# Stick-breaking attention: logits one step earlier, running sums split on VectorE, 13 equal steps

## The chip, the cores and the metric

The kernel runs on one core of one Trainium2 chip. The metric is the device time of one execution in microseconds; the median of several executions counts. Five engines work side by side: TensorE (PE, with its weight loads PEld) for matrix products, VectorE (DVE) and ScalarE (ACT) for elementwise work, GpSimd (POOL) for masks, and SyncE (SP), which issues the transfers from memory.

## What is computed

Two decoder layers over 512 tokens of width 2048, in float32. The first layer is sparse softmax attention, the second is stick-breaking attention; each is followed by an output product, a layer norm and a gated embedding. The change lies in the second layer's attention:

```python
q, gate = jnp.split(x @ w_in, [WIDTH_B], axis=-1)
...
z = jnp.einsum('bqngd,bsnd->bngqs', qg, k).astype(jnp.float32) * (HEAD_DIM ** -0.5)
strict = key_pos[None, :] < t[:, None]
log_om = jnp.where(strict, -jax.nn.softplus(z), 0.0)
suffix = lax.cumsum(log_om, axis=log_om.ndim - 1, reverse=True) - log_om
a = jnp.where(strict, jnp.exp(jax.nn.log_sigmoid(z) + suffix), 0.0)
o = jnp.einsum('bngqs,bsnd->bqngd', a.astype(v.dtype), v)
...
return (o * jax.nn.silu(gate)) @ w_o
```

There are 16 query heads in 4 groups; the four heads of a group share one key and value head.

## The kernel before

Activations are kept transposed, features on partitions and tokens along the free axis. Every float32 operand of a product is split into a high and a low part in a reduced format (`split`, L131: ScalarE rounds the high part, VectorE subtracts for the low part), and a product is three matmuls (`mm3`, L135). Weights arrive by transfers into `raw`, are split into `wh` and `wl` two items ahead, and are used by four gate units each.

The second layer's attention runs group by group (`for g in range(4)`, L1344). In each group two streams of work are woven together on TensorE, whose order is the order of the program:

- the **gate product** of the group (`gemm_w`), 64 units of three matmuls into banks 0 to 3; at every fourth unit the next weight item is split;
- **`sticks(g, Q)`** (L1241), the attention. A unit u = (i, kb) is the 128 queries of block i for all four heads against key block kb; there are ten units, (0,0), (1,1), (1,0), (2,2), (2,1), (2,0), (3,3), (3,2), (3,1), (3,0), from the diagonal (kb = i) back to key block 0.

For a unit, `logits` (L1252) makes z = K Q on TensorE, then softplus: for kb > 0 VectorE copies z to `a`; ScalarE takes Abs, Exp and Ln in `wk`; VectorE adds into `sp`. A diagonal unit is masked on GpSimd (`strict`) and split into `sh` and `sl` at once; any other unit waits for the total of the unit before it. `weights` (L1284) multiplies `sh` and `sl` with a triangle of ones. For kb > 0 the sums go into the bank `later`, VectorE adds them to the copy of z (`a`), and `carry` (L1274) adds the total's row of `later` into `sp` of unit u + 1, which is then split; for kb = 0 the sums are added onto z in its own bank (L1297). ScalarE takes the exponential, a diagonal unit is masked, and the result is split into one of two pairs `A`. `values` (L1305) multiplies with V into the bank `o`, and after kb = 0 ScalarE copies `o` out.

The loop at L1313 makes 12 steps: in step s the logits of unit s, the weights of unit s - 1, the values of unit s - 2, with a `yield` after each. `interleave` (L57) runs a share of gate units after each yield: 52 units over 34 yields in groups 1 to 3, behind a lead of 8; 46 over 28 in group 0, of which 18 units have run already. Four extra yields in step 1 hold back the first weights.

The order on TensorE is written out; on the other engines a scheduler orders instructions by its own estimate of when each is ready. Where `pinned` is set (through `paced`, L325), `keep_in_program_order` ties an instruction to the one traced just before it on the same engine: it is issued after that one, while instructions that are not pinned may still be put between or ahead. Background pieces from the list `bg` are run one after a gate unit and are pinned: in groups 0 to 2 the splits of the next group's queries (`split_scaled`, L1208, `c<-f` in the profile), in group 0 also the pieces of `restore`.

Of the kernel before, what the change touches and what calls it, by code (L numbers as in the profile page):

```python
# [10 lines left out]
F32 = mybir.dt.float32  # L11
F32R = mybir.dt.float32r
I32 = mybir.dt.int32
AF = mybir.ActivationFunctionType
ALU = mybir.AluOpType
# [31 lines left out]
def run(gen):  # L47
    for _ in gen:
        pass


def steps(gen, n):
    for _ in range(n):
        next(gen, None)


def interleave(main, n_main, fill, n_fill, lead=0):  # L57

    steps(fill, lead)
    done = 0  # L60
    for i, _ in enumerate(main, 1):
        steps(fill, n_fill * i // n_main - done)
        done = n_fill * i // n_main
    run(fill)
# [13 lines left out]
def trunk_kernel(  # L78
# [39 lines left out]
    act, dve, pool = (Paced(e) for e in (nc.scalar, nc.vector, nc.gpsimd))  # L118
# [9 lines left out]
    def bank(i, name="ps"):  # L128
        return psum.tile([128, 512], F32, name=name, tag=f"bank{i}")

    def split(hi, lo, src, eng=dve):  # L131
        act.activation(hi, src, AF.Copy)
        eng.tensor_tensor(lo, src, hi.bitcast(F32), ALU.subtract)
# [155 lines left out]
    def gemm_w(items, get, banks, n=512, order=range(NK)):  # L289

        for i, kb in enumerate(order):
            wh, wl = next(items)
            x = get(kb)
            for j, out in enumerate(banks):
                a, b = j * 128, min(n, (j + 1) * 128)
                mm3(out[: b - a], (wh[:, a:b], wl[:, a:b]), x, i == 0, i == len(order) - 1)
                yield
# [27 lines left out]
    def paced(fn, *args):  # L325
        was, pinned[0] = pinned[0], True
        fn(*args)
        pinned[0] = was
# [4 lines left out]
    def pumped_at(gen, when):  # L333
        for i, _ in enumerate(gen):
            if bg and i in when:
                one()
            yield

    def pumped(gen, every=1):

        for i, _ in enumerate(gen):
            if bg and i % every == 0:
                one()
            yield
# [199 lines left out]
    for k in (4, 5, 6, 7, None, 0, None, 1, 2, 3):  # L544
        if k is None:
            first = 4 * (units[-1][1] == 0)
# [113 lines left out]
    def first_pair(banks):  # L660
        for k2 in range(NK // 2):
            for outs, get in zip(banks, (late_plain, plain)):
                for kb in (2 * k2, 2 * k2 + 1):
                    wh, wl = next(items)
                    for j, out in enumerate(outs):
                        s = slice(j * 128, (j + 1) * 128)
                        mm3(out, (wh[:, s], wl[:, s]), get(kb), kb == 0, kb == NK - 1)
                        yield
# [7 lines left out]
    gemm = first_pair((banks, kbanks))  # L676
    steps(gemm, 48)
    gemm = pumped(gemm, 2)
# [26 lines left out]
    gemm = gemm_w(items, late_plain, banks)  # L705
# [41 lines left out]
    def split_queries(g):  # L747
        Q = []
        for h in range(4):
            q = tuple(pkv.tile([128, T], F32R, name=f"q{s}", tag=f"q{s}", bufs=4) for s in "hl")  # L750
            split(*q, F[g][:, h])
            Q.append(q)
        return Q
# [55 lines left out]
    Q = split_queries(0)  # L809
# [59 lines left out]
    for g in range(4):  # L869
        banks = mm_banks("g")  # L870
        interleave(attend(g, Q), 36, gemm_w(items, plain, banks), 50 - 6 * (g == 0), lead=8 + 6 * (g == 0))
        if g < 3:
            Q = split_queries(g + 1)
        for h in range(4):
            sg = pb.tile([128, T], F32, name="sg", tag="sg", bufs=3)
# [286 lines left out]
    Q, A = ([tuple(spots[n : n + 2]) for n in where] for where in ((10, 12, 16, 18), (20, 22)))  # L1162
# [7 lines left out]
    with tc.tile_pool(name="sp", bufs=1) as sp:  # L1170
        Kf, Vf = shared
        banks = [bank(b, "k") for b in range(4)]
        gemm = gemm_w(kitems, plain, banks, order=PAIRS)
# [11 lines left out]
        for n, dst in enumerate((Vf, *F)):  # L1185
            M = product_banks(4 - n)
            gemm = pumped_at(gemm_s(items, C3, M), (13, 20, 27, 34, 41, 53, 65, 77, 89, 101))
# [18 lines left out]
    px = pc_.enter_context(ss(name="px", bufs=1))  # L1206
# [16 lines left out]
    def log_exp():  # L1223
        tc.keep_in_program_order(act.preload_act_table_set("natural_log_exp_and_others"))

    def work():
        return px.tile([128, 512], F32, name="wk", tag="wk", bufs=4)

    def strict(ap, i):
        v = ap.rearrange("p (h q) -> p h q", h=4)  # L1230
# [10 lines left out]
    def sticks(g, Q):  # L1241
        units = [(i, kb) for i in range(4) for kb in range(i, -1, -1)]
        state = {}
        waiting = {}
        out = {}

        def parts_of(sp):
            parts = tuple(px.tile([128, 512], F32R, name=f"s{s}", tag=f"s{s}", bufs=2) for s in "hl")
            split(*parts, sp)
            return parts  # L1250

        def logits(u):  # L1252
            i, kb = units[u]
            z = bank(4 + u % 2, "z")
            ks = slice(kb * 128, (kb + 1) * 128)
            mm3(z, [k[:, ks] for k in K[g]], Q[i], True, True)
            e = work()
            sp = px.tile([128, 512], F32, name="sp", tag="sp", bufs=2)
            if kb:

                copy = px.tile([128, 512], F32, name="a", tag="a", bufs=3)
                dve.tensor_copy(copy, z)
            act.activation(e, z, AF.Abs)
            act.activation(e, e, AF.Exp, scale=-1.0)
            act.activation(e, e, AF.Ln, bias=1.0)
            dve.scalar_tensor_tensor(sp, z, 0.0, e, ALU.max, ALU.add)
            z = copy if kb else z
            if kb == i:
                strict(sp, i)
                state[u] = z, parts_of(sp)  # L1270
            else:
                waiting[u] = z, sp

        def carry(u, total):  # L1274

            z, sp = waiting.pop(u)
            if units[u][1] % 2:
                dve.tensor_tensor(sp[0:1], sp[0:1], total[0:1], ALU.subtract)
            else:
                rows = slice(96, 128)  # L1280
                dve.scalar_tensor_tensor(sp[rows], total[rows], ident[rows, 127:128], sp[rows], ALU.mult, ALU.add)
            state[u] = z, parts_of(sp)

        def weights(u):  # L1284
            i, kb = units[u]
            z, parts = state[u]
            a = z if kb else work()
            if kb:
                later = bank(6, "later")
                for n, p in enumerate(parts):  # L1290
                    pe.matmul(later, down if kb % 2 else tri, p, start=n == 0, stop=n == 1)
                dve.tensor_tensor(a, z, later, ALU.subtract if kb % 2 else ALU.add)
                carry(u + 1, later)
                act.activation(a, a, AF.Exp)
            else:
                for n, p in enumerate(parts):
                    pe.matmul(z, tri, p, start=False, stop=n == 1, skip_group_check=True)  # L1297
                act.activation(a, z, AF.Exp)
            if kb == i:
                strict(a, i)  # L1300
            parts = A[u % 2]
            split(*parts, a)
            state[u] = parts

        def values(u):  # L1305
            i, kb = units[u]
            if kb == i:
                out[i] = bank(7, "o")
            mm3(out[i], [v[:, g * 128 : (g + 1) * 128] for v in V[kb]], state.pop(u), kb == i, kb == 0)
            if kb == 0:  # L1310
                act.activation(F[g][:, :, i * 128 : (i + 1) * 128], out[i].rearrange("p (h q) -> p h q", h=4), AF.Copy)

        for s in range(12):  # L1313

            done = [i for n, (i, kb) in enumerate(units) if kb == 0 and s == max(n + 3, 0 if g else 8)]
            if g < 3:
                bg.extend(lambda i=i: split_scaled(g + 1, i) for i in done)
            for fn, u in ((logits, s), (weights, s - 1), (values, s - 2)):
                if 0 <= u < 10:
                    fn(u)  # L1320
                    yield
                if g and s == 1 and fn == logits:
                    for _ in range(4):
                        yield

    log_exp()

# [7 lines left out]
    gemm = pumped(chunk)  # L1335
    first = sticks(0, Q)
    for n in (9, 1):
        steps(gemm, n)
        steps(first, 1)
    bg.extend(lambda i=i: split_scaled(0, i) for i in (2, 3))  # L1340
    steps(gemm, 8)
    gemm = pumped(chunk, 2)

    for g in range(4):  # L1344
        if g:
            log_exp()
            banks = mm_banks("g")
            gemm = pumped(gemm_w(items, plain, banks))
        if 0 < g < 3:
            bg.append(lambda g=g: split_keys(g + 1))  # L1350
        if g:
            interleave(sticks(g, Q), 30 + 4, gemm, 52, lead=8)
        else:
            interleave(first, 30 - 2, gemm, 64 - 18)
        drain()
        if g < 3:
            split_scaled(g + 1, 3)
        for h in range(4):
            sg = work()
            act.activation(sg, banks[h], AF.Silu)  # L1360
            dve.tensor_tensor(F[g][:, h], F[g][:, h], sg, ALU.mult)
    pk_.close()
# [55 lines left out]
```

## Time and profile before

| | |
|---|---|
| median of three runs | 1887.99 us (1886.46 to 1888.04) |
| profiled execution | 1886.27 us, span 1884.1 us |
| granted TensorE clock | 1.000 |
| TensorE busy | 1860.9 us, 99% |
| VectorE busy | 1222.8 us, 65% |
| ScalarE busy | 944.0 us, 50% |
| stick-breaking stage | about 1234 to 1510 us of the span |

In the rows shown below, a line names the engine, the source line, the operation, and output and inputs by the program's tile names; [..] behind a row is the idle time of that engine before it and what ended it. Most VectorE and ScalarE instructions bear the line of a helper (L111), so they are told apart by their tiles: `sp<-z,wk` is the softplus sum, `sp<-later,ident,sp` and `sp<-sp,later` are the carry, `a<-a,later` the add of the sums, `c<-a` the split of the weights into `A` (and `c<-wk` for kb = 0). Matmuls overlap, so their pace is read from start to start. In the rows by stretch the columns are the stretch, its length, and busy time (with instruction counts) of PE, PEld, DVE, ACT, POOL, then the granted clock, the share of the transfer engines and GB/s.

### The profile page before, as it was taken

The page shows a single profiled execution, that of the slowest core. Times are in us where ns is not written, and L with a number is a line of the kernel's source. Part 1 is how long each engine was busy: PE and PEld are TensorE (multiplying, and loading weights), DVE is VectorE, ACT ScalarE, POOL GpSimd, SP SyncE. Part 2 cuts the span into 40 slices and gives each one's busy share as a digit, 9 for nine tenths or more (in the row PEclk, how much of TensorE's full clock was granted, in tenths as well). Part 3 has the DMA queues.
Part 4 walks back from the last instruction along what each step waited for, and adds up shares of the span by engine and source line. Part 5 has one row for each costly group of instructions (what it writes and reads, how often), then busy time and mean ns, then how long its engine had stood idle before and what let it go on. Part 6 is the DMA issues. An engine that isn't in the chain of part 4 may idle for free.

```text
span 1884.1 us, 24811 instructions
## 1 busy us (share of the span) xinstructions
PE 1860.9 (99%) x9181; PEld 1575.1 (84%) x9181; DVE 1222.8 (65%) x2363; ACT 944.0 (50%) x1712; POOL 27.4 (1%) x48
## 2 busy tenths in 40 slices
PE   9999999999999999999999999999999999999998
PEld 8898888888888888888888999977777788888887
DVE  5768678567565455675377888877766645567534
ACT  3546423455554432474245444477877743246422
POOL 0000000000000000000000000000000000000000
PEclk9999999999999999999999999999999999999999
DMA  6442333312222532333343333322122152242333
GB/s 196 126 123 62 96 101 90 101 56 68 73 66 63 182 98 78 123 101 115 103 145 112 105 99 107 107 85 78 56 68 60 53 190 94 79 129 90 123 101 112
DMA packets 111178, 189.21 MB, mean 100 GB/s; under 512 B 8528, under 2 KB 29008, under 8 KB 111056
## 3 DMA queue, kind: packets, MB, share of 16 engines
q1 hardware_dynamic: 111056, 187.62, 32.3%
q8 instruction: 72, 1.18, 0.3%
q14 instruction: 50, 0.41, 0.1%
HBM read 179.21 MB, written 8.39 MB: 100 GB/s over the span
## 4 chain that ended last, share of the span: by engine, by line
PE 95%; DVE 3%; ACT 2%; issue 0%; DMA 0%; SPq 0%; POOL 0%; DVEq 0%
PE g L136 12%; PE g L137 12%; PE g L138 12%; PE o L138 7%; PE o L136 7%; PE o L137 7%; PE m L136 4%; PE m L137 4%; PE m L138 4%; PE q L136 3%; PE q L137 3%; PE q L138 3%; PE k L138 2%; PE k L137 2%; PE k L136 2%; PE iq L138 1%
## 5 line engine op out<-in xcount | busy, mean ns | idle before, releaser
L111 ACT ACTIVATE wh<-raw 128x512 fp32r<-128x512 f32 (+3 forms) x685 | 397.8, 581 | 703.6 <-PE g L137 235.5
L111 DVE TENSOR_TENSOR wl<-raw,wh 128x512 fp32r<-128x512 f32 (+3 forms) x685 | 432.0, 631 | 472.8 <-ACT wh L111 457.6
L136 PE MATMUL g<-xh,wh 128*128 128x512 f32 x1024 | 404.1, 395 | 0.1
L138 PE MATMUL g<-xh,wl 128*128 128x512 f32 x1024 | 399.9, 391 | 0.0
L137 PE MATMUL g<-xl,wh 128*128 128x512 f32 x1024 | 399.6, 390 | 0.0
L138 PEld LDWEIGHTS g<-xh,wl 128*128 128x128 f32 x1024 | 192.3, 188 | 41.0
L136 PEld LDWEIGHTS g<-xh,wh 128*128 128x128 f32 x1024 | 192.5, 188 | 37.4 <-ACT wk L111 0.7
L137 PEld LDWEIGHTS g<-xl,wh 128*128 128x128 f32 x1024 | 192.6, 188 | 37.1
L138 PE MATMUL o<-xh,wl 128*128 128x512 f32 x512 | 199.4, 389 | 0.0
L136 PE MATMUL o<-xh,wh 128*128 128x512 f32 x512 | 199.3, 389 | 0.0
L137 PE MATMUL o<-xl,wh 128*128 128x512 f32 x512 | 199.3, 389 | 0.0
L138 PEld LDWEIGHTS o<-xh,wl 128*128 128x128 f32 x512 | 96.1, 188 | 20.4 <-DVE wl L111 0.5
L136 PEld LDWEIGHTS o<-xh,wh 128*128 128x128 f32 x512 | 96.1, 188 | 19.9
L137 PEld LDWEIGHTS o<-xl,wh 128*128 128x128 f32 x512 | 96.1, 188 | 19.8
L136 PE MATMUL q<-xh,wh 128*128 128x512 f32 x256 | 99.7, 389 | 0.0
L138 PE MATMUL q<-xh,wl 128*128 128x512 f32 x256 | 99.6, 389 | 0.0
L137 PE MATMUL q<-xl,wh 128*128 128x512 f32 x256 | 99.6, 389 | 0.0
L111 ACT ACTIVATE sh<-st 128x512 fp32r<-128x512 f32 x80 | 49.7, 624 | 44.3 <-DVE st L111 44.2
L111 DVE TENSOR_TENSOR sl<-st,sh 128x512 fp32r<-128x512 f32 x80 | 55.2, 690 | 13.9 <-ACT sh L111 13.9
L111 DVE TENSOR_TENSOR xl<-f,xh 128x512 fp32r<-128x512 f32 x80 | 54.3, 686 | 12.6 <-ACT f L111 12.3
L138 PEld LDWEIGHTS q<-xh,wl 128*128 128x128 f32 x256 | 48.1, 188 | 10.1
L136 PEld LDWEIGHTS q<-xh,wh 128*128 128x128 f32 x256 | 48.1, 188 | 10.0
(294 smaller groups left out, 3342.9 us busy)
## 6 DMA issues: line engine op xcount, KB each, us to landing
raw<-w_in_a SPq DMA_DIRECT2D x95, 512.0 KB, 3.6
raw<-w_in_b SPq DMA_DIRECT2D x64, 512.0 KB, 3.8
raw<-w_ple_gate SPq DMA_DIRECT2D x52, 512.0 KB, 3.6
raw<-w_o_a SPq DMA_DIRECT2D x24, 512.0 KB, 3.8
raw<-w_o_b SPq DMA_DIRECT2D x24, 512.0 KB, 3.7
raw<-w_kv_b SPq DMA_DIRECT2D x16, 512.0 KB, 3.8
raw<-w_ple_gate SPq DMA_DIRECT2D x24, 256.0 KB, 2.9
f<-xT SPq DMA_DIRECT2D x4, 1024.0 KB, 6.6
```

The costliest lines, as they stand in the source:

```text
L111: ins = method(*args, **kw)
L136: pe.matmul(out, a[0], b[0], start=start, stop=False)
L137: pe.matmul(out, a[0], b[1], start=False, stop=False)
L138: pe.matmul(out, a[1], b[0], start=False, stop=stop)
```

## The change

- The loop makes 13 steps: logits of unit s, weights of unit s - 2, values of unit s - 3. Every step has three yields, whether a part runs or not; step 1 has two extra yields in groups 1 to 3 in place of four. The gate units are spread over 39 + 2 yields in groups 1 to 3 and over 39 - 6 in group 0.
- z goes into bank 4 for kb > 0, into bank 5 for kb = 0, and into bank 6 for the first unit; `sp` reads the copy of z where there is one. Buffers: `wk` 3 in place of 4, `sp` 3 in place of 2, `a` 4 in place of 3; the silu of the gate uses the tag `a`.
- In `carry` the high part is a VectorE copy in place of ScalarE's, right behind the sum, and the low part follows. Diagonal units are still split by `split`.
- `carry` comes ahead of the add into `a`, and both are paced.
- With 13 steps the background split of query block 3 is also listed in step 12; the call after the group stays.

```diff
     def work():
-        return px.tile([128, 512], F32, name="wk", tag="wk", bufs=4)
+        return px.tile([128, 512], F32, name="wk", tag="wk", bufs=3)
...
         def logits(u):
             i, kb = units[u]
-            z = bank(4 + u % 2, "z")
+
+            z = bank(4 if kb else 5 if u else 6, "z")
...
-            dve.scalar_tensor_tensor(sp, z, 0.0, e, ALU.max, ALU.add)
+            dve.scalar_tensor_tensor(sp, copy if kb else z, 0.0, e, ALU.max, ALU.add)
             z = copy if kb else z
             if kb == i:
                 strict(sp, i)
-                state[u] = z, parts_of(sp)
+                state[u] = z, new_parts()
+                split(*state[u][1], sp)
...
-            state[u] = z, parts_of(sp)
+            hi, lo = new_parts()
+            dve.tensor_copy(hi, sp)
+            dve.tensor_tensor(lo, sp, hi.bitcast(F32), ALU.subtract)
+            state[u] = z, (hi, lo)
...
-                dve.tensor_tensor(a, z, later, ALU.subtract if kb % 2 else ALU.add)
-                carry(u + 1, later)
+                paced(carry, u + 1, later)
+                paced(dve.tensor_tensor, a, z, later, ALU.subtract if kb % 2 else ALU.add)
                 act.activation(a, a, AF.Exp)
...
-        for s in range(12):
+        for s in range(13):
 
             done = [i for n, (i, kb) in enumerate(units) if kb == 0 and s == max(n + 3, 0 if g else 8)]
...
-            for fn, u in ((logits, s), (weights, s - 1), (values, s - 2)):
+            for fn, u in ((logits, s), (weights, s - 2), (values, s - 3)):
                 if 0 <= u < 10:
                     fn(u)
+                yield
+                if g and s == 1 and fn == logits:
                     yield
-                if g and s == 1 and fn == logits:
-                    for _ in range(4):
-                        yield
+                    yield
...
     for n in (9, 1):
         steps(gemm, n)
-        steps(first, 1)
+        steps(first, 3)
...
-            interleave(sticks(g, Q), 30 + 4, gemm, 52, lead=8)
+            interleave(sticks(g, Q), 39 + 2, gemm, 52, lead=8)
         else:
-            interleave(first, 30 - 2, gemm, 64 - 18)
+            interleave(first, 39 - 6, gemm, 64 - 18)
...
-            sg = work()
+            sg = px.tile([128, 512], F32, name="sg", tag="a", bufs=4)
```

More of the change, by code (lines that the diff above doesn't have):

```diff
@@ L1245, in sticks, with new_parts @@
         out = {}
[L1247 to L1250, printed above, removed]
+        def new_parts():
+            return tuple(px.tile([128, 512], F32R, name=f"s{s}", tag=f"s{s}", bufs=2) for s in "hl")
         def logits(u):
             i, kb = units[u]
-            z = bank(4 + u % 2, "z")
+            z = bank(4 if kb else 5 if u else 6, "z")
             ks = slice(kb * 128, (kb + 1) * 128)
@@ L1257, in logits @@
             e = work()
-            sp = px.tile([128, 512], F32, name="sp", tag="sp", bufs=2)
+            sp = px.tile([128, 512], F32, name="sp", tag="sp", bufs=3)
             if kb:
-                copy = px.tile([128, 512], F32, name="a", tag="a", bufs=3)
+                copy = px.tile([128, 512], F32, name="a", tag="a", bufs=4)
                 dve.tensor_copy(copy, z)
```

## The prediction

> **What bounds the kernel now.** I read the page first, for the engine that fills the span.
>
> ```profile
> span 1884.1 us, 24811 instructions
> PE 1860.9 (99%) x9181; PEld 1575.1 (84%) x9181; DVE 1222.8 (65%) x2363; ACT 944.0 (50%) x1712; POOL 27.4 (1%) x48
> ```
>
> TensorE is 99% busy, so an edit pays or costs only by the TensorE waits it takes away or makes. The second view, who waited for whom on TensorE, puts nearly all waits into the stick-breaking stage (columns: us in total, times, longest):
>
> ```profile
> PE z L1297 <- DVE sl L111: 5.3, 8, 1.1
> PE later L1291 <- ACT sh L111: 5.0, 5, 1.8
> PE later L1291 <- DVE sl L111: 4.2, 9, 1.2
> PE z L1297 <- ACT sh L111: 1.4, 2, 0.7
> ```
>
> All four end at a high or low part of the running sums (`sh`, `sl`): 15.9 us. The third view gives busy times by stretch, here one stretch for each of the four K/V groups:
>
> ```profile
> 1233.70:1307.00 73.30, 67.96 (x288) 53.03 (x287) 57.25 (x94) 58.19 (x106) 5.78 (x10) 1.00 0.26 80
> 1307.00:1374.70 67.70, 63.89 (x271) 49.98 (x271) 47.76 (x74) 52.59 (x92) 6.19 (x8) 1.00 0.20 62
> 1374.70:1442.30 67.60, 63.96 (x273) 50.34 (x272) 47.19 (x73) 52.51 (x91) 6.20 (x8) 1.00 0.20 63
> 1442.30:1510.00 67.70, 63.67 (x272) 50.13 (x271) 45.21 (x70) 50.60 (x89) 5.80 (x8) 1.00 0.20 63
> ```
>
> The fourth, TensorE's timeline, gives the pace:
>
> ```profile
> 1399.66 0.40 PE L136 MATMUL g<-xh,wh 128*128 128x512 f32 x1
> ...
> 1404.44 0.39 PE L1291 MATMUL later<-sh,down 128*128 128x512 f32 x1
> 1404.99 0.50 PE L1291 MATMUL later<-sl,down 128*128 128x512 f32 x1 [0.16 <-DVE sl L111]
> 1405.33 0.40 PE L136 MATMUL g<-xh,wh 128*128 128x512 f32 x1
> ```
>
> Between the first two rows stand 21 starts (gate 3, values 3, gate 6, logits 3, gate 6): 4.78 / 21 = 0.2276 us each. After a wait the next start comes 0.34 later, so a wait costs about 0.11 more. By the code a group has 272 matmuls (64 gate units of 3; 10 units with 3 logits, 2 sums, 3 values): 61.9 us at this pace, against 67.7. The first stretch has 288 records, 65.5 of 73.3. The stage loses 7.8 + 5.8 + 5.7 + 5.8 = 25.1 us. No cure of these waits can bring more.
>
> **The change, part by part.** *Less cover in a step.* Gate units per step fall from 3 x 52/34 = 4.6 to 3 x 52/41 = 3.8. With 8 matmuls of its own, a step on TensorE shrinks from 4.95 to 4.4 us: every chain that runs from one step to the next has half a microsecond less.
>
> *The pins.* `carry` and the add into `a` are now paced: each VectorE instruction of theirs goes behind the VectorE instruction traced just before. The trace of before shows what such a pin does, since the background split of the next group's queries (`c<-f`) carries one:
>
> ```profile
> 1403.04 0.69 DVE L111 TENSOR_TENSOR wl<-raw,wh 128x512 fp32r<-128x512 f32 x1 [0.53 <-ACT wh L111]
> 1403.65 0.68 DVE L111 SCALAR_TENSOR_TENSOR c<-f,c 128x512 fp32r<-128x512 f32 x1
> 1404.25 0.69 DVE L111 TENSOR_TENSOR sl<-sp,sh 128x512 fp32r<-128x512 f32 x1
> ...
> 1406.41 0.69 DVE L111 SCALAR_TENSOR_TENSOR sp<-z,wk 128x512 f32<-128x512 f32 x1 [0.20 <-ACT wk L111]
> 1407.14 0.76 DVE L111 SCALAR_TENSOR_TENSOR sp<-later,ident,sp 32x512 f32<-32x512 f32 x1
> ```
>
> Here a weight split `wl` was traced between the logits and the `c<-f`, so `c<-f` sits behind `wl` and ahead of that step's `sp`. Where no `wl` lies between, `c<-f` sits right behind the logits' last instruction, as the next block shows in its last row. It is a diagonal unit from its third logits matmul on (copy, Abs, `sp`, GpSimd's mask, `sh`, `sl`):
>
> ```profile
> 1392.08 0.39 PE L138 MATMUL z<-c,c 128*128 128x512 f32 x1
> 1392.64 0.69 DVE L111 COPY a<-z 128x512 f32<-128x512 f32 x1
> 1393.49 0.58 ACT L111 ACTIVATE wk<-z 128x512 f32<-128x512 f32 x1
> 1395.77 0.69 DVE L111 SCALAR_TENSOR_TENSOR sp<-z,wk 128x512 f32<-128x512 f32 x1 [1.25 <-ACT wk L111]
> 1396.59 0.96 POOL L1232 TENSOR_SCALAR_AFFINE_SELECT sp<-sp 128x512 f32<-128x512 f32 x1 [5.38 <-DVE sp L111]
> 1397.59 0.63 ACT L111 ACTIVATE sh<-sp 128x512 fp32r<-128x512 f32 x1 [1.33 <-POOL sp L1232]
> 1398.59 0.68 DVE L111 TENSOR_TENSOR sl<-sp,sh 128x512 fp32r<-128x512 f32 x1
> 1399.19 0.68 DVE L111 SCALAR_TENSOR_TENSOR c<-f,c 128x512 fp32r<-128x512 f32 x1
> ```
>
> So `sp` starts 3.7 us and `sl` 6.5 us after that matmul. In the changed step the order of tracing is logits(s), fill, weights(s-2) with its pinned carry. In steps 3 and 6 the logits are of a diagonal unit (i=2, i=3), weights is unit 1 or 4, and both have a carry. No weight split falls between: a split is traced at every fourth gate unit, and counting 52i/41 from a lead of 8 the gate units there are numbers 21, 22 and 33. So the carry, whose total lies ready at 1.1 to 1.6 us, waits until 6.5 + 0.6 = 7.1, the 0.6 being the spacing of independent VectorE operations above. Behind it wait the high part, the low part, the add into `a`, and then TensorE twice: for the next sums and for the values. Before, no carry fell into these steps (they had unit 2 or 5, with kb = 0), and none was pinned.
>
> *The high part on VectorE.* The row of such a cast, and of what leaves ScalarE:
>
> ```profile
> L111 DVE CAST xh<-raw 128x512 fp32r<-128x512 f32 x1 | 0.4, 419 | 0.0
> ...
> L111 ACT ACTIVATE sh<-sp 128x512 fp32r<-128x512 f32 x40 | 24.9, 623 | 9.2 <-POOL sp L1232 6.6 <-DVE sp L111 2.5
> ```
>
> 24 of the 40 move: 24 x 0.42 = 10 us more VectorE work in the whole stage, which has 15 to 20 us a group free; no cost by itself. Chain of a carry: 0.76 + 0.03, cast 0.42 + 0.03, low part 0.69, and 0.05 to TensorE (`sl` ends at 1404.94, its matmul starts at 1404.99): 1.98 us. The dependent step costs 0.73 (1406.41 to 1407.14), the independent one 0.60. The Trainium skill ("VectorE: DVE Perf Modes", The DRAIN you can't avoid) has it that a semaphore between chained VectorE operations costs nothing extra; the rows differ by 0.13, and by the page the three-operation chain would be 0.4 shorter and the time some 3 us less. I take the rows.
>
> *The add into `a` behind carry and parts.* From the add to the values' low part:
>
> ```profile
> 1389.10 0.69 DVE L111 TENSOR_TENSOR a<-a,later 128x512 f32<-128x512 f32 x1 [0.81 <-PE later L1291]
> 1389.82 0.63 ACT L111 ACTIVATE a<-a 128x512 f32<-128x512 f32 x1
> 1390.58 0.63 POOL L1232 TENSOR_SCALAR_AFFINE_SELECT a<-a 128x512 f32<-128x512 f32 x1 [3.68 <-ACT a L111]
> 1391.25 0.63 ACT L111 ACTIVATE c<-a 128x512 fp32r<-128x512 f32 x1 [0.19 <-POOL a L1232]
> 1391.91 0.69 DVE L111 TENSOR_TENSOR c<-a,c 128x512 fp32r<-128x512 f32 x1
> ```
>
> 0.72 + 0.76 + 0.67 + 0.66 + 0.69 + 0.05 = 3.55 with GpSimd's mask, 0.77 less without (`ea` straight to the split).
>
> *Site A, steps 3 and 4.* From the third logits matmul: carry 7.1, low part 8.35, its matmul at 9.1, `a` at 8.95, the second matmul of values(1) at 12.5 (unit 1 is diagonal: masked). On TensorE that is matmul number 33, due at 7.5. Delay 5.0, of it 2.7 at the sums and 2.3 at the values, + 0.1. In groups 1 and 2 a background split stands between (as 1399.19 does): + 0.6.
> *Site C, steps 6 and 7.* Values(4) unmasked: ready at 11.7, matmul 30 due at 6.8: 4.9 + 0.1. Step 5's carry, behind its `sp`, delays values(3) by some 2 us, but after the logits of step 6, so inside this sum.
> *Site D, steps 8 to 10.* In groups 1 to 3 a weight split lies between, the carry starts at about 2.6, and only the late `a` shows: 0.4 to 0.5 three times, 1.5 with restarts.
> Group 0 (1.39 units a yield): 5.1 at A; at C a restore adds 0.4 but three more matmuls cover: 4.7; at D no split lies between: 2.5.
> Sum 12.3 + 12.3 + 12.2 + 11.6 = 48.4 us. Some 2 us of waits at the first logits stay; the old 25.1 go: + 25 us if nothing else queues in these chains. In the rows above `wl` and `c<-f` stood in front of `sl`, so I add one foreign VectorE operation (0.6) and one on ScalarE (0.5) at each of 8 sites: + 9, an estimate. Net + 34 us. Bounds: if `sl` comes 0.6 sooner, with less on ScalarE, and nothing queues, + 20; if one of the two sites in every group hides, with its queueing, about + 10; with twice the queueing, + 43.
>
> *At nothing:* all z in bank 4 (Abs ends at 1394.07, 2.0 us after the matmul; the next z comes 3.4 or more after it; were Abs 1.4 later, TensorE would wait); `wk`, `a`, `sp` buffers (each next use is a step or more behind the release); the second split of query block 3 in step 12 (one ScalarE and one VectorE operation in three groups, under the next group's 8 gate units, 5.5 us; uncovered, 2 us for each group).
>
> The profiled execution took 1886.27 us; the median shown is 1887.99, 1.7 above. 1887.99 + 34 = 1922.
>
> **The rivals.** *Faster: carries go at once.* If the carry comes when its total lands (the diagonal's chain ends early enough, or the pin doesn't hold it), a carry is done by 1.6 + 2.0 = 3.6 us, against matmuls due at 5.5 or later: the old waits vanish, and site D and the first logits stay, 4 x 1.5 + 2 = 8 of 25.1. Time 1888 - 17 = 1871. It decides where `sl` of units 3 and 6 ends before about 4 us. For it: it is just the slack that a second step ahead gives, and ScalarE loses 24 operations. Against: `sp` alone starts at 3.7, and `c<-f` at 1399.19 shows the pin holding.
> *No change:* delays at A and C half as long, 1888.
> *Slower still: a cold TensorE.* Waits of 2.7 to 3.4 us at A and C, where the longest now is 1.8. The start of the trace shows a cold pace:
>
> ```profile
> 4.42 0.52 PE L137 MATMUL iq<-xl,wh 128*128 128x384 f32 x1
> 4.75 0.52 PE L138 MATMUL iq<-xh,wl 128*128 128x384 f32 x1
> ...
> 6.46 0.34 PE L136 MATMUL iq<-xh,wh 128*128 128x384 f32 x1
> 6.64 0.34 PE L137 MATMUL iq<-xl,wh 128*128 128x384 f32 x1
> ```
>
> 0.33 against 0.18, until 5.7 us. A stretch of 4 us at that pace loses 2 us: over four sites + 8, over eight + 16: 1930 to 1938. Against: the granted clock is 1.00 in all four stretches. The Trainium skill ("TensorE: Matmul & The Clock Gate", HAM oscillation) warns of idle gaps over about 3.4 us; these waits reach that edge, and no run here shows one.
>
> **How the numbers follow.** Forecast 0.80, colder 0.05, no change 0.04, faster 0.11. A measurement of this kernel can tell about 0.2% (3.8 us). Slower is 0.85. The range 1898 to 1943 runs from the bound of one hidden site a group (1888 + 10) over twice the queueing (1931) and the cold case (1938) to a little of both; outside lie the faster and the unchanged case and a little of the forecast's own tail.
>
> **What would show it.** Right: in the list of TensorE's waits new rows for `o` (values) waiting on `c`, and for `z` L1297 with waits over 2 us, some 3 to 5 us a group each; on VectorE's timeline the carry right behind the diagonal's `sl`; the group stretches at 72 to 78 us instead of 67.7; DVE CAST at 0.42. Wrong: stretches of 63 to 66 us, or carries that start within 1 us of their total in steps 3 and 6.

## The result and the profile after

The changed kernel takes 1946.13 us (median of 4 runs, 1945.98 to 1947.78) against 1887.74 us: a ratio of 1.0313, 95% interval 1.0295 to 1.0331. It is 58 us slower; + 34 was forecast and 1946 lies just above the range's end of 1943. The page's head, with the row of the granted clock in 40 slices:

```profile
span 1944.4 us, 24849 instructions
PE 1886.6 (97%) x9181; PEld 1585.8 (82%) x9181; DVE 1235.3 (64%) x2390; ACT 932.7 (48%) x1691; POOL 25.6 (1%) x48
...
PEclk9999999999999999999999999999989899999999
```

The span grew by 60.3 us, VectorE's work by 12.5. TensorE has the same instructions and is "busy" longer: the clock row shows why in two slices. TensorE's waits:

```profile
PE o L136 <- ACT c L111: 17.8, 15, 2.2
PE z L1300 <- DVE sh L111: 14.6, 4, 4.0
PE later L1294 <- DVE a L111: 8.6, 5, 3.7
PE o L137 <- DVE c L111: 6.5, 15, 0.7
PE z L1300 <- DVE sl L111: 2.7, 6, 0.6
```

Here are the rows that were forecast as a sign: values waiting on `c` (24.3 us in 30 waits) and the sums at L1300 with waits of 3 to 4 us. These five lines are 50.2 us; the four of before were 15.9. The stretches of the four groups, the first cut at its first gate unit, the others 2 to 3 us ahead of their first logits, as before:

```profile
1233.70:1322.30 88.60, 73.14 (x291) 55.14 (x291) 60.53 (x101) 55.49 (x101) 5.96 (x10) 0.96 0.22 66
1322.30:1406.00 83.70, 71.12 (x273) 53.44 (x272) 51.55 (x82) 50.13 (x87) 5.41 (x8) 0.92 0.17 51
1406.00:1489.00 83.00, 71.01 (x275) 53.62 (x274) 50.75 (x80) 49.94 (x86) 5.41 (x8) 0.92 0.17 51
1489.00:1572.00 83.00, 71.65 (x278) 54.25 (x277) 49.56 (x78) 48.54 (x85) 5.41 (x8) 0.92 0.17 51
```

83 us a group in place of 67.7 (72 to 78 was forecast), and a granted clock of 0.92 to 0.96 in place of 1.00. At half clock for the missing share, that is 88.6 x 0.08 + 249.7 x 0.16 = 47 us of the stage.

Sites A and C are the prediction's two places of a group where a carry falls behind a diagonal's logits. Site A of the last group shows the whole mechanism. VectorE's timeline from the diagonal's low part on:

```profile
1510.10 0.69 DVE L111 TENSOR_TENSOR sl<-sp,sh 128x512 fp32r<-128x512 f32 x1 [1.18 <-ACT sh L111]
1510.80 0.76 DVE L111 SCALAR_TENSOR_TENSOR sp<-later,ident,sp 32x512 f32<-32x512 f32 x1
1511.59 0.69 DVE L111 SCALAR_TENSOR_TENSOR sp<-a,wk 128x512 f32<-128x512 f32 x1
1512.20 0.42 DVE L111 CAST sh<-sp 128x512 fp32r<-128x512 f32 x1
1512.66 0.69 DVE L111 TENSOR_TENSOR sl<-sp,sh 128x512 fp32r<-128x512 f32 x1
1513.38 0.69 DVE L111 TENSOR_TENSOR a<-a,later 128x512 f32<-128x512 f32 x1
```

And TensorE's, from the diagonal unit's last logits matmul on:

```profile
1503.27 0.39 PE L138 MATMUL z<-c 128*128 128x512 f32 x1
...
1505.08 0.39 PE L1294 MATMUL later<-sl,down 128*128 128x512 f32 x1
...
1512.68 0.79 PE L1300 MATMUL z<-sh,tri 128*128 128x512 f32 x1 [3.13 <-DVE sh L111]
1513.40 0.79 PE L1300 MATMUL z<-sl,tri 128*128 128x512 f32 x1
...
1517.85 0.80 PE L137 MATMUL o<-c,c 128*128 128x512 f32 x1
1518.44 0.63 PE L138 MATMUL o<-c,c 128*128 128x512 f32 x1
1518.87 0.63 PE L136 MATMUL g<-xh,wh 128*128 128x512 f32 x1
1519.30 0.63 PE L137 MATMUL g<-xl,wh 128*128 128x512 f32 x1
```

The total was on its way at 1505.08; the carry starts at 1510.80, right behind the diagonal's `sl`, 7.5 us after the logits (forecast 7.1). A foreign `sp` slips in behind it, so the three are not adjacent. At all eight sites A and C of this trace the carry stands behind the diagonal's `sl`, 6.4 to 8.3 us after the logits. The values' second matmul comes at 14.6 where 7.5 was its turn. And the last rows are 0.43 apart in place of 0.23: the gate products, which wait for nothing, run at half pace. The stretch of that place:

```profile
1511.80:1522.00 10.20, 7.74 (x16) 5.05 (x17) 4.10 (x7) 3.00 (x6) 0.63 (x1) 0.50 0.17 54
```

A clock of 0.50 for 10.2 us, from just before the end of a 3.1 us wait. I split every start in the stage, from the first gate unit (1233.7) to just behind the last group's values, by what it lost against 0.2276 us. Starts behind a wait lost 22.1 us before and 65.0 after (+ 42.9), starts at half pace with no wait 0 and 16.8, all others 4.2 and 4.0. That is 59.5 of the 60.3 us. By place, over the four groups:

| place (from, to) | before | after |
|---|---|---|
| site A (logits of unit 3 to values of unit 1) | 4.6 | 29.8 |
| site C (logits of unit 6 to values of unit 4) | 2.6 | 28.5 |
| behind C to the last values | 14.6 | 20.1 |
| between A and C | 2.4 | 6.2 |
| the rest (first logits, group ends) | 2.1 | 1.2 |

### The profile page after: what moved, and what is told of

Read it like the earlier page. It is cut to its first block, busy times and chain, and to the rows that moved or that the text cites. A ratio compares the mean times of both kernels' runs of the same rounds, so it can differ in the third digit from the quotient of the medians.

```text
span 1944.4 us, 24849 instructions
## 1 busy us (share of the span) xinstructions
PE 1886.6 (97%) x9181; PEld 1585.8 (82%) x9181; DVE 1235.3 (64%) x2390; ACT 932.7 (48%) x1691; POOL 25.6 (1%) x48
## 5 line engine op out<-in xcount | busy, mean ns | idle before, releaser
L138 PEld LDWEIGHTS o<-xh,wl 128*128 128x128 f32 x512 | 96.1, 188 | 20.1 <-DVE wl L111 0.2
L111 DVE TENSOR_TENSOR xl<-f,xh 128x512 fp32r<-128x512 f32 x80 | 54.3, 686 | 12.5 <-ACT f L111 12.2
L111 ACT ACTIVATE wk<-z 128x512 f32<-128x512 f32 x56 | 33.1, 591 | 51.6 <-DVE a L111 22.9
L137 PEld LDWEIGHTS q<-xl,wh 128*128 128x128 f32 x256 | 48.0, 188 | 10.1
```

The source lines that it names most:

```text
L111: ins = method(*args, **kw)
L137: pe.matmul(out, a[0], b[1], start=False, stop=False)
L138: pe.matmul(out, a[1], b[0], start=False, stop=stop)
```

## The experiments

Each ratio is against the kernel before, run on the same chip.

**The pins alone.** The changed kernel without them:

```diff
-                paced(carry, u + 1, later)
-                paced(dve.tensor_tensor, a, z, later, ...)
+                carry(u + 1, later)
+                dve.tensor_tensor(a, z, later, ...)
```

> The changed kernel without the two pins: carry and the add into a are no longer tied to the VectorE instruction traced before them; all else stays (13 steps, high part on VectorE, carry ahead of the add). Pins theory: with no pin the carry starts within about 1 us of its total in steps 3 and 6 instead of behind the diagonal's sl, TensorE's waits fall from 50.9 us to under 15, the clock stays at 1.00, and the time is 1868 to 1885. Rival, VectorE overloaded by the 24 casts or too little cover in 13 equal steps: the waits stay, 1935 to 1950. In between (1890 to 1930) both have a part.

Measured: 1894.49 us, 1.0035 (1.0022 to 1.0049). 52 of the 58 us go with the pins, so neither the casts nor the cover make the loss. But the time is above what the theory gave, and still 0.35% slower than before. Most of TensorE's waits are now at L1300:

```profile
PE z L1300 <- DVE sl L111: 11.8, 8, 1.9
PE z L1300 <- DVE sh L111: 5.0, 5, 2.1
PE o L137 <- DVE c L111: 1.9, 3, 1.5
```

VectorE's timeline at site A of the last group says what they wait for:

```profile
1466.87 0.76 DVE L111 SCALAR_TENSOR_TENSOR sp<-later,ident,sp 32x512 f32<-32x512 f32 x1
1467.66 0.69 DVE L111 TENSOR_TENSOR a<-a,later 128x512 f32<-128x512 f32 x1
1468.27 0.69 DVE L111 TENSOR_TENSOR wl<-raw,wh 128x512 fp32r<-128x512 f32 x1
1468.87 0.68 DVE L111 SCALAR_TENSOR_TENSOR sp<-a,wk 128x512 f32<-128x512 f32 x1
1469.55 0.69 DVE L111 COPY a<-z 128x512 f32<-128x512 f32 x1
1470.15 0.44 DVE L111 CAST sh<-sp 128x512 fp32r<-128x512 f32 x1
```

The carry goes at once, but the order that the scheduler then chose puts four other operations between it and its high part. That is a cost of its own, which the forecast's faster rival left out. The clock has a part in it too: the span is 8.6 us longer than before, and by the count above the starts at half pace lost 5.8 us.

**Weights ahead of logits**, the pins kept:

```diff
-            for fn, u in ((logits, s), (weights, s - 2), (values, s - 3)):
+            for fn, u in ((weights, s - 2), (logits, s), (values, s - 3)):
```

> The changed kernel with weights(s-2) traced ahead of logits(s) in each step; the pins stay. Pins theory: the pin now sits behind work of the step before, not behind this step's logits, so the waits at z and o vanish and the time is 1866 to 1885. Rival, the pinned chain of carry, high, low and add is itself too long: the values still wait on c, 1900 to 1930. Rival, too little cover: 1935 or more.

Measured: 1894.82 us, 1.0041 (1.0026 to 1.0056), in none of the three ranges. Pins, casts, depth and cover are those of the changed kernel; only what is traced in front of the carry differs, and 51 us go. So the harm is the tie to the diagonal's logits. What is left is mostly the values:

```profile
PE o L137 <- DVE c L111: 9.0, 12, 1.2
PE o L136 <- ACT c L111: 3.2, 6, 1.1
```

**The pins in the old order** (12 steps, add first, then carry, both paced).

> The kernel before with the two pins alone (add first, then carry, both paced; 12 steps, ScalarE makes the high part). Pins theory in its narrow form, that a pin costs only where it ties a carry to a diagonal unit's logits: in the 12-step order no carry falls into such a step, so within 6 us of before, 1882 to 1894. Rival, pins cost in any order: 1900 or more.

Measured: 1904.59 us, 1.0091 (1.0076 to 1.0106). The narrow theory fell: pins cost 17 us in the 12-step order too. The waits:

```profile
PE later L1291 <- ACT sh L111: 15.4, 12, 2.1
PE later L1291 <- DVE sl L111: 3.9, 13, 0.4
```

There the add into `a` is tied behind `sp` of the same step, and the carry behind the add; so a pin behind `sp`, which waits for a chain of its own, costs too. Some 10 of the 17 us are starts at half pace.

**Zero matmuls in TensorE's waits.** They add a product with zeros:

```diff
+                if u == 2:
+                    warm(z, 16)
                 for n, p in enumerate(parts):
                     pe.matmul(z, tri, ...)
...
+            if u == 4:
+                warm(out[i], 8)
```

> The changed kernel with matmuls of a zero matrix added, 16 ahead of the sums of unit 2 and 8 ahead of the values of unit 4 in each group: they add nothing to the result and stand where TensorE waits now (3.6 us and 1.8 us at 0.23 each). Cold-clock theory, that about 20 us of the loss is TensorE at half clock after these waits: the waits are filled, the clock rows go back towards 1.00 and the time falls to 1922 to 1932. Rival, the slow pace has another cause (weights or operands late): no shorter than 1944, or longer by what of the 22 us of zero matmuls finds no room.

Measured: 1943.41 us, 1.0296 (1.0279 to 1.0313): neither theory's number. 96 zero matmuls are 21.9 us of added work, and only 18 us of waits (65.0 to 47.0) took them in. The clock did go up, over the stage from 0.93 to 0.96:

```profile
1233.70:1572.00 338.30, 302.95 (x1220) 231.93 (x1219) 213.24 (x342) 205.16 (x358) 22.19 (x34) 0.96 0.18 55
```

Starts at half pace lost 9.8 us in place of 16.8. The sum - 18.0 + 21.9 - 7.0 + 0.5 = - 2.6 is the 2.7 measured. So filling waits does keep the clock, but by 7 us, not by the 14 or more that I had expected.

**Add first, logits first.** The changed kernel with its two paced calls turned round:

```diff
-                paced(carry, u + 1, later)
                 paced(dve.tensor_tensor, a, z, later, ...)
+                paced(carry, u + 1, later)
```

> The changed kernel with the order of the two paced calls turned round: add into a first, then carry (logits still first). Theory of the prediction: the add and the carry both wait behind the diagonal's sl; the add first frees the values by 1.3 us but the sums come 0.6 later, so the second wait of each site shrinks and the first stays: 1915 to 1935, waits 40 to 50 us in place of 65. If the order of these two is the main thing: under 1900. If it is nothing: 1940 to 1950.

Measured: 1929.63 us, 1.0224 (1.0210 to 1.0238), as forecast. No wait at the values remains in the list; those at the sums grow:

```profile
PE z L1300 <- DVE sh L111: 27.2, 8, 5.3
PE later L1294 <- DVE sl L111: 6.7, 8, 1.1
```

So the add's place behind the carry is worth 16 us, and the tie to the logits holds without it.

**The high part back on ScalarE**, pins kept (`act.activation(hi, sp, AF.Copy)` in `carry`).

> The changed kernel with the carry's high part back on ScalarE, the pins kept (carry, low part, add). Rival theory, the 24 casts overload VectorE or ScalarE was the better place: well under 1946, 1900 to 1930. Pins theory alone: the carry still waits behind the diagonal's sl, so the waits stay, and a hop to ScalarE and back adds 0.3 us a site: 1940 to 1955.

Measured: 1944.72 us, 1.0303 (1.0289 to 1.0317). The casts are not the cause; the 24 of them cost VectorE 10.0 us in the changed kernel, as forecast:

```profile
L111 DVE CAST sh<-sp 128x512 fp32r<-128x512 f32 x24 | 10.0, 418 | 0.1
```

**The carry free, the rest of its chain tied.** High part, low part and add stay paced, the first instruction isn't.

> The changed kernel with the carry's first instruction free and the high part, low part and the add still pinned one behind the other. Pins theory in its exact form, that the tie of the first instruction to the logits does the harm and the ties within the chain none: as without pins or better, 1880 to 1896. Rival, the ties of the high part, low part and add hold back the values: 1900 to 1930.

Measured: 1930.62 us, 1.0225 (1.0209 to 1.0240), a miss: only 15 us go, about where the rival had it. VectorE's timeline at site A of the last group:

```profile
1495.93 0.76 DVE L111 SCALAR_TENSOR_TENSOR sp<-later,ident,sp 32x512 f32<-32x512 f32 x1
...
1499.21 0.42 DVE L111 CAST sh<-sp 128x512 fp32r<-128x512 f32 x1
1500.47 1.29 DVE L111 TENSOR_TENSOR sl<-sp,sh 128x512 fp32r<-128x512 f32 x2 [0.85 <-ACT sh L111]
1501.68 0.68 DVE L111 TENSOR_TENSOR a<-a,later 128x512 f32<-128x512 f32 x1
```

The carry starts 2.3 us after the logits (1493.64), so the first tie did hold it. But a pin only says "behind", not "next to": the high part was put 3.3 us later, the low part beside the diagonal's, and the add, tied behind the low part, still comes at 8 us. The run without pins has its high and low part at the same places of this site (5.6 and 7.4 us after the logits); only its add goes at 3.1 us. By these rows the tie of the add behind the low part makes most of the 36 us between the two runs. Why the scheduler puts the high part there in both, with nothing in the trace to wait for, stays open.

**Both repairs: weights first and add first, paced.**

> Weights ahead of logits as in the earlier run, and the add into a ahead of carry again; both paced. If what was left there (12 us of values waiting on c) comes from the add standing behind carry, high and low part, those waits go: waits under 16 us, 1872 to 1882, faster than before. Rival, the pinned chain as a whole or VectorE's load holds it: 1890 to 1900, as with weights first alone.

Measured: 1887.58 us, 0.9998 (0.9989 to 1.0007). All 58 us are accounted for, but nothing is won, where 1872 to 1882 was expected. The values' waits are gone but for 0.6 us; the sums wait as before:

```profile
PE z L1300 <- DVE sl L111: 6.5, 10, 0.7
PE z L1300 <- DVE sh L111: 4.2, 7, 1.6
PE later L1294 <- DVE sl L111: 1.8, 6, 0.7
PE later L1294 <- DVE sh L111: 1.8, 4, 0.7
```

**More cover.** That kernel, then the kernel before, with 56 gate units spread in place of 52, then the first of them without pins:

```diff
-            interleave(sticks(g, Q), 39 + 2, gemm, 52, lead=8)
+            interleave(sticks(g, Q), 39 + 2, gemm, 56, lead=8)
```

> Weights first and add first, pinned, with all 56 gate units that follow the lead of 8 spread over the 41 yields in groups 1 to 3 (52 before, the last 4 behind): 4.1 units a step in place of 3.8. If the waits left there are a chain that is too long for its step by a few tenths, 0.2 us more cover in each of some 8 steps takes 1 to 1.6 us a group: 1881 to 1885, faster than both kernels. If what is left is not a matter of cover: 1886 to 1889.

> The kernel before with 56 in place of 52 gate units over its 34 yields, nothing else. Cover theory: its chain from sums to sums misses its step by 0.5 to 1.5 us in some steps; 0.24 us more in each of 8 steps takes 1 to 2 us a group: 1881 to 1886. If cover is not what it lacks: 1886 to 1889.

> As the run with weights first, add first and 56 units, without the pins. If pins help once weights come first (they keep carry, high and low part together): 1886 to 1896, slower than with them. If pins only harm: 1878 to 1884.

Measured: 1884.22 us, 0.9979 (0.9970 to 0.9987); 1882.16 us, 0.9970 (0.9960 to 0.9981); 1883.17 us, 0.9976 (0.9967 to 0.9985). All three beat both kernels, and the lowest time, within the intervals of the other two, has the kernel before with one number changed: the last four gate units, which ran behind the attention where nothing waits, are worth more inside it. With more cover, pins and no pins are the same within their intervals. The old kernel's list then reads:

```profile
PE later L1291 <- DVE sl L111: 5.2, 6, 1.5
PE z L1297 <- DVE sl L111: 4.3, 8, 1.1
PE later L1291 <- ACT sh L111: 2.4, 3, 1.8
PE z L1297 <- ACT sh L111: 1.6, 3, 0.7
```

13.5 us in place of 15.9. That is half of the 4.7 us by which the span is shorter; the rest lies in starts that lose too little each to stand in this list.

## Why the prediction was right and wrong

- *The mechanism was right*: pinned behind the logits of a diagonal unit, the carry starts at 7.5 us (forecast 7.1) at site A of the last group, behind the diagonal's `sl` at all eight sites, and what is traced ahead of it is worth 51 us. So were the casts at no cost (0.418 us each) and the bank and buffer edits, on which at most 0.7 us of TensorE's waits fall (`g` on `sg`). On chained VectorE operations, where I held to the rows against the Trainium skill ("VectorE: DVE Perf Modes", The DRAIN you can't avoid), the rows after agree with those of before: the low part starts 0.46 us behind the high part, whose duration is 0.42, so it waits for its end.
- *The step that failed is the cold TensorE*: I gave it a chance of 0.05 because the clock was 1.00 in all stretches of before, and left it out of the sum. It measured 16.8 us of starts at half pace, in eight falls of the clock: the price that I had set for "over eight sites" (16). The old trace could not speak against it: its longest wait was 1.8 us and the change was to make waits of 2.7 to 3.4. With it, + 34 would have been + 51. The trace's stage grew by 59.5, 25 more than forecast: 16.8 are this, 5.6 are waits (65.0, where the sum had 48.4 + 2 + 9), and some 3 are small losses between matmuls, which the sum let go with the old 25.1 and which stayed (4.2 before, 4.0 after).
- *Sites A and C were sized about right, by an allowance*: 21.6 + 19.7 bare, + 9 for foreign operations, make 50.3. Of the 58.3 measured 52.5 are starts behind a wait and 4 starts at half pace. The 9 was a guess and not a working; that it came out near is luck. Where one foreign VectorE operation was allowed for, the last group's site A shows one in front of the high part, and the low part's matmul at 10.1 instead of 9.1; the values then came at 14.6 instead of 12.5.
- *Site D was undersized*: 7 us forecast from behind C to the last values, 20.1 measured, where before had 14.6. Waits are 11.1 of it and starts at half pace 7.2. I had let the old waits there vanish, but a late `a` took their place: in the first group the sums wait 3.7 us for the add, in the others the values wait for `c`, 1.3 us a group.
- *The faster rival* (1871) was mispriced too: without the pins the time is 1894; there the scheduler parts the carry from its high part, and the clock falls too.

## What to carry to other kernels

A pin "behind the last instruction traced on this engine" inherits the whole wait of whatever that instruction happens to be; ask at each place where it lands, and trace the urgent chain ahead of the slow one. When a change makes TensorE waits that add up to 1.7 us or more within some 3.4 us, price the clock as well as the wait. And before a pipeline is made deeper, look for work that lies outside it uncovered: here four gate units moved into the attention brought 0.3%, the deeper pipeline nothing.

## What the runs showed of the hardware

TensorE fell to half clock after waits shorter than I had thought. The Trainium skill ("TensorE: Matmul & The Clock Gate", HAM oscillation) puts the danger at idle gaps over about 3.4 us; the runs here differ. The run without pins has no wait over 2.1 us, and yet a clock of 0.50:

```profile
1259.80:1266.60 6.80, 5.64 (x14) 4.26 (x14) 3.86 (x7) 2.88 (x7) 0.00 (x0) 0.50 0.15 39
```

It begins with the end of the 2.1 us wait and takes in another of 1.2 us. The weights-first run has no wait over 1.2 us in the stage, and it falls too, behind two waits of 1.15 and 0.85 us close together:

```profile
1260.11:1263.53 3.42, 1.42 (x6) 0.64 (x5) 2.93 (x7) 3.30 (x7) 0.00 (x0) 1.00 0.07 11
1263.53:1266.94 3.41, 3.41 (x10) 2.66 (x9) 1.48 (x3) 0.00 (x0) 0.00 (x0) 0.50 0.42 142
```

TensorE was busy for 1.42 of the 3.42 us ahead of this fall. Idle time within such a stretch, and not the longest wait, is what goes with a fall in these traces. In each of them the changes of the granted clock lie whole multiples of 3.41 us apart, and every half-clock piece of the stage lasts 3.41, 6.83 or 10.24 us. Cut at that step, the traces hold 52 falls ahead of the kernel's end. In 51 of them TensorE was idle for 1.68 us or more of the 3.41 us ahead, in one for 1.40. No stretch at full clock with another behind it has more than 1.69 us idle. The kernel before, with single waits of up to 1.8 us, has at most 1.56 us idle in a stretch, and its clock stays at 1.00 through the stage. So about half of a stretch is what a fall takes here, as far as idle time can be read where the ends of matmuls are modelled. A start at half clock lost 0.2 us for each 512-column matmul. In the changed kernel the starts at half pace lost 16.8 us in the 47 us at half clock, 0.36 us for each.
